# Query products in three fp32r passes and feed-forward entries on the un-normed input, in a three-block kernel on one Trainium2 core

## The chip, the core and the metric

One NeuronCore of a Trainium2 chip runs the whole program. The time is the device time of one execution in microseconds (us). The profiled execution has a time of its own, and its span (first to last instruction) is a little shorter than that.

## What is computed

The reference runs three transformer-like blocks on 256 tokens of width 1024, with 256 context tokens beside them in the first block, all in fp32. Cut to the parts that matter here:

```
mod = silu(c) @ ada_w[i] + ada_b[i]            # six vectors per block
h   = rmsnorm(x, norm1_g) * (1 + sc1) + sh1    # hc: the same of ctx
# block 0: differential attention on h and hc; block 1: short convolution
x   = x + g1 * mixer(h, hc)
x   = x + g2 * swiglu(rmsnorm(x, norm2_g) * (1 + sc2) + sh2, w_in, w_out)
# block 2: state space branch + pooling branch, then a mixture of 64 experts
```

The hidden width of both feed-forward networks (FFN) is 2816, so `w_in` is 1024 x 5632. Everything the change touches lies in the first 560 us: the query projection of block 0, and the entries to the FFN of blocks 0 and 1.

## The kernel before, in words

**Products.** Activations are held transposed, as eight tiles of 128 features by 256 tokens. An fp32 product is made as three fp32r matmuls on TensorE (`mm3`, L280 to L282): weight high part by activation high part, weight high by activation low, weight low by activation high. A weight unit (128 x 1024, eight stationary tiles) is loaded by SP into `st`, its high part `wh` is written by ScalarE (ACT, L146) and its low part `wl` by VectorE (DVE, L134). The object `st` streams the units: `take(n)` gives the next n tiles and splits some units ahead, `split_to` and `more` split further ahead, and the split instructions stand in ACT's and DVE's queue where they are issued. Ring buffers hold five split units.

**The Q stage (L591 to L660).** A loop over the eight feature tiles n adds tile n's share to the queries. It uses no split: `st.raw()` hands out the raw weights and `full`, an fp32 copy of the modulated x, and TensorE runs 8 plain fp32 matmuls for each n (L625; each leaves two records in the trace). Between them stand the products and column sums (`products`, `columns`, L504 to L524) that make the modulation vectors of a tile two ahead: 16 records into `pa`, a copy of `pa` by ACT (`pa_s`, L515), and two small matmuls into `raw` (named `ms` in the trace). `modulate_x(n + 1)` makes tile n + 1 on DVE and ACT during step n: two small sums into `ab` (L492, L493), `na` (L529), `full` (L532), `hH` (L533) and `hL` (L534). The context tile is modulated the same way by `modulate_c`, one or two tiles a step from n = 3. GpSimd (POOL) is idle there. The K stage follows, with split weights and a moving tile of 512 columns (x and context).

**The entries to the FFNs.** `residual` (L880 ff.) makes the eight output tiles of a projection and adds them to x. `done` are tiles made before it, `sums` adds up squares for the norm. For the second FFN it also feeds a `Raw` object: `Raw.split(n)` writes x times the norm's gain, un-normed, as high and low part `u`, so that products can start before the norm is known. `Raw.run` (L934 ff.) makes the first four output tiles on `u`, all four at each feature tile k, and corrects them with the row factors afterwards. The first FFN has no `Raw` before the change: it sums the squares (L351), makes 1/sqrt on DVE (L289 to L321), spreads it over rows (L363), modulates (`na` L379, `hh` L380, `hl` L383), and only then starts the products. In the background DVE works off matrix-vector units `ada` (L395), at a rate `bg_pace` for each unit of weights taken; `b.hold` keeps them back.

Of the kernel before, what the change touches and what calls it, by code (L numbers as in the profile page):

```python
# [107 lines left out]
class Stream:  # L108
# [129 lines left out]
class Builder:  # L238
# [186 lines left out]
def build(ctx, tc, ap):  # L425
# [100 lines left out]
    def modulate(src, rows, n, i, full=None):  # L526

        t = b.wk.tile([P, T], F32, tag="na", name="na", bufs=3)
        nc.vector.scalar_tensor_tensor(t, src[n], AB[n][:, 1, i:i + 1], rows, op0=ALU.mult, op1=ALU.mult)  # L529
        yield  # L530
        if full is not None:
            nc.scalar.activation(full, t, AF.Identity, bias=AB[n][:, 0, i:i + 1])  # L532
        nc.scalar.activation(hH[:, n, 1 - i], t, AF.Identity, bias=AB[n][:, 0, i:i + 1])  # L533
        nc.vector.scalar_tensor_tensor(hL[:, n, 1 - i], t, AB[n][:, 0, i:i + 1], hH[:, n, 1 - i], op0=ALU.add, op1=ALU.subtract)  # L534
        yield

    for n in ks:
        AB[n] = cp.tile([P, 2, 2], F32, name=f"ab{n}")
# [56 lines left out]
    ready, fulls = [], {}  # L595

    def modulate_x(n):
        finish_x(n)
        fulls[n] = b.wk.tile([P, T], F32, tag="rp_b", name="full", bufs=2)
        for _ in modulate(xs, rows_x, n, 0, fulls[n]):  # L600
            pass

    def modulate_c():
        todo = []
        for i in ready[:2]:
            finish_c(i)
            todo.append(modulate(cx, rows_c, i, 1))
            next(todo[-1])
        del ready[:2]
        for o in todo:  # L610
            next(o)

    modulate_x(0)
    for n in ks:
        w = st.raw()
        for i in range(KD):
            if i == 2 and n + 1 < KD:
                modulate_x(n + 1)
# [13 lines left out]
        ready.append(n)  # L632
        if n >= 3:
            modulate_c()
# [9 lines left out]
        if n >= KD - 2:  # L644
            st.nu = max(st.nu, KD)
            st.split_to(n + 3)
    while ready:
        modulate_c()
# [238 lines left out]
    def residual(ktiles, xh, xl, gate, sums, done=(), raw=None):  # L887
# [10 lines left out]
        for n in range(KD):  # L898
            if n < len(done):
                ps = done[n]  # L900
            else:
                b.hold = raw is not None and n == KD - 1
# [6 lines left out]
                if raw and n == KD - 1:  # L909
# [7 lines left out]
    class Raw:  # L917
# [3 lines left out]
        def __init__(self, A, B, pool, tag):  # L921
            self.A, self.B = A, B
# [1391 lines left out]
```

## Time and profile before

| | |
|---|---|
| time, median of 3 runs | 1554.79 us (1552.02 to 1555.33) |
| the profiled execution: time, span | 1555.31 us, 1553.5 us |
| mean granted TensorE clock | 0.989 of full speed |
| busy: TensorE, VectorE, ScalarE, GpSimd | 95%, 63%, 43%, 18% |
| Q stage, first product to first product of K | 20.9 to 62.1 us |
| first FFN, end of the residual to its 144th matmul | 232.3 to 258.0 us |
| second FFN, the same | 520.2 to 550.65 us |

A row of the timeline is: start, duration, engine, line, operation, output and inputs, shape, count, and in brackets the engine's idle time before it and what ended that. A row of a group ends with busy time, mean duration, and idle time before it. A row of windows has, after the stretch and its length, the busy time (and instructions) of PE, PEld, DVE, ACT and POOL, then the granted clock, the DMA share and GB/s; filtered by a tile it has only the engines that touch that tile.

### The profile page before, as it was taken

To read this page: it belongs to the slowest core of one execution; us is meant where nothing else is said; L and a number is where in the kernel's file an instruction comes from. 1 tells how busy PE (TensorE), PEld (TensorE's weight loads), DVE (VectorE), ACT (ScalarE), POOL (GpSimd) and SP (SyncE) were. 2 spreads that over 40 slices of the span, in tenths; PEclk is the share of its full clock that TensorE was granted. 3 is DMA by queue.
4 is the path that set the end of the run, shared out by engine and by line. 5 is a ranking of instruction groups with operands and counts; after the bars stand their busy time and mean duration, and the time that the engine had idled before them with its cause. 6 is when DMAs were issued, how large, how long until landed. Compare 5 with 4: busy or idle time off the path is not lost. (4 is left out here: it accounts for less than half of the span.)

```text
span 1553.5 us, 28280 instructions
## 1 busy us (share of the span) xinstructions
PE 1483.4 (95%) x11184; PEld 1189.5 (77%) x11184; DVE 986.0 (63%) x1850; ACT 669.0 (43%) x1175; POOL 274.2 (18%) x439
## 2 busy tenths in 40 slices
PE   6999898999999899999899999999999999999996
PEld 4789588999999899999899998999634444444332
DVE  3698858887888788796988867565423333323332
ACT  3523645444454454453677765343322222222222
POOL 0070560000100100021067668001100000000000
PEclk9999999999999899998999999999999999999999
DMA  9678215987956479786354554677489999999995
GB/s 375 232 244 273 94 69 210 340 333 283 355 201 235 172 263 350 290 325 241 126 176 162 178 176 145 218 277 301 188 303 412 420 420 420 421 420 420 421 420 215
DMA packets 71429, 431.93 MB, mean 278 GB/s; under 512 B 8176, under 2 KB 8688, under 8 KB 28416
## 3 DMA queue, kind: packets, MB, share of 16 engines
q1 hardware_dynamic: 68656, 422.77, 70.9%
q0 software_dynamic: 1344, 4.80, 0.9%
q10 hardware_dynamic: 1296, 2.55, 0.5%
q8 instruction: 88, 1.44, 0.4%
q14 instruction: 45, 0.37, 0.1%
HBM read 429.01 MB, written 1.08 MB: 277 GB/s over the span
## 5 line engine op out<-in xcount | busy, mean ns | idle before, releaser
L134 DVE TENSOR_TENSOR wl<-st,wh 128x1024 fp32r<-128x1024 f32 x294 | 365.0, 1250 | 70.4 <-ACT wh L146 70.1
L146 ACT ACTIVATE wh<-st 128x1024 fp32r<-128x1024 f32 x294 | 306.2, 1055 | 109.7 <-PE ps_r L281 41.9
L280 PE MATMUL ps_f<-hh,wh 128*128 128x256 f32 x672 | 189.2, 282 | 1.7 <-ACT hh L380 1.3
L282 PE MATMUL ps_f<-hh,wl 128*128 128x256 f32 x672 | 189.1, 281 | 0.7 <-DVE wl L134 0.7
L281 PE MATMUL ps_f<-hl,wh 128*128 128x256 f32 x672 | 189.0, 281 | 0.1
L395 DVE SCALAR_TENSOR_TENSOR ada<-ada,crow 128x1024 f32<-128x1024 f32 x128 | 164.5, 1293 | 20.4 <-DMA ada<-in_ada 20.4
L340 POOL TENSOR_TENSOR sq<-sq 128x256 f32<-128x256 f32 x30 | 38.9, 1303 | 577.8 <-ACT sq L338 577.4
L280 PEld LDWEIGHTS ps_f<-hh,wh 128*128 128x128 f32 x672 | 127.2, 189 | 2.2 <-ACT hh L380 1.5
L282 PEld LDWEIGHTS ps_f<-hh,wl 128*128 128x128 f32 x672 | 127.1, 189 | 1.0 <-DVE wl L134 1.0
L281 PEld LDWEIGHTS ps_f<-hl,wh 128*128 128x128 f32 x672 | 127.1, 189 | 0.4 <-DVE hl L383 0.4
L280 PE MATMUL ps_ssd<-hh,wh 128*128 128x256 f32 x352 | 101.4, 288 | 0.0
L281 PE MATMUL ps_r<-gL,wh 128*128 128x256 f32 x352 | 98.7, 280 | 0.0
L280 PE MATMUL ps_r<-gH,wh 128*128 128x256 f32 x352 | 98.7, 280 | 0.0
L282 PE MATMUL ps_r<-gH,wl 128*128 128x256 f32 x352 | 98.7, 280 | 0.0
L282 PE MATMUL ps_ssd<-hh,wl 128*128 128x256 f32 x352 | 98.6, 280 | 0.0
L281 PE MATMUL ps_ssd<-hl,wh 128*128 128x256 f32 x352 | 98.6, 280 | 0.0
L1818 DVE TENSOR_SCALAR xb<-gtp,A,mod 128x256 f32<-128x256 f32 (+2 forms) x52 | 27.3, 526 | 111.3 <-ACT xb L1816 111.2
L1816 ACT ACTIVATE xb<-gtp,mod,A 128x256 f32<-128x256 f32 (+2 forms) x52 | 28.5, 549 | 118.5 <-PE gtp L1836 118.4
L1806 POOL TENSOR_TENSOR WG<-G,pwq 128x256 f32<-128x256 f32 (+2 forms) x24 | 14.1, 607 | 363.5 <-DVE G L1802 363.5
L1836 PEld LDWEIGHTS gtp<-G,utH 128*128 128x128 f32 x208 | 39.2, 188 | 45.9 <-DVE xb L1818 19.7
L274 ACT ACTIVATE oH<-wr 128x512 fp32r<-128x512 f32 (+2 forms) x53 | 33.4, 630 | 92.9 <-DVE wr L2094 80.3
L280 PEld LDWEIGHTS ps_ssd<-hh,wh 128*128 128x128 f32 x352 | 66.3, 188 | 1.0 <-issue 1.0
(616 smaller groups left out, 4167.7 us busy)
## 6 DMA issues: line engine op xcount, KB each, us to landing
st<-in_ws SPq DMA_DIRECT2D x151, 1024.0 KB, 6.5
ada<-in_ada SPq DMA_DIRECT2D x128, 512.0 KB, 5.0
w<-in_we SPq DMA_DIRECT2D x40, 1024.0 KB, 19.8
w_st<-in_we SPq DMA_DIRECT2D x40, 1024.0 KB, 19.8
w_y<-in_we SPq DMA_DIRECT2D x32, 1024.0 KB, 19.8
w_ut<-in_we SPq DMA_DIRECT2D x30, 1024.0 KB, 19.8
w_h<-in_we SPq DMA_DIRECT2D x21, 1024.0 KB, 19.8
x<-in_we SPq DMA_DIRECT2D x10, 1024.0 KB, 19.8
```

The lines of the kernel that those rows point to most:

```text
L134: self.b.nc.vector.tensor_tensor(lo.rearrange("p a c -> p (a c)"), w, h.rearrange("p a c -> p (a c)"), op=ALU.subtract)
L146: nc.scalar.activation(h.rearrange("p a c -> p (a c)"), w, AF.Copy)
L274: self.nc.scalar.activation(h, src, AF.Copy)
L280: nc.tensor.matmul(out, lhsT=h[:, k], rhs=xh, start=start, stop=False, skip_group_check=True)
L281: nc.tensor.matmul(out, lhsT=h[:, k], rhs=xl, start=False, stop=False, skip_group_check=True)
L282: nc.tensor.matmul(out, lhsT=lo[:, k], rhs=xh, start=False, stop=stop, skip_group_check=True)
L340: nc.gpsimd.tensor_tensor(self.acc[tag], self.acc[tag], sq, op=ALU.add)
L395: self.nc.vector.scalar_tensor_tensor(junk, w, 1.0, crow, op0=ALU.mult, op1=ALU.mult, accum_out=dst[:, j:j + 1])
L1806: nc.gpsimd.tensor_tensor(cut(WG, tt), cut(G, tt), ws_[:, tt][:, :, None].to_broadcast([P, n, c]), op=ALU.mult)
L1816: nc.scalar.activation(out[:, k, :n], tp[:, i, :n], AF.Identity, scale=A, bias=B)
L1818: nc.vector.tensor_scalar(out[:, k, :n], tp[:, i, :n], A, B, op0=ALU.mult, op1=ALU.add)
L1836: nc.tensor.matmul(tp[:, i, :n], lhsT=hl_[:, tt, k * P:(k + 1) * P], rhs=G[:, tt, :n], start=(i == 0 and tt == 0 and hl_ is utH), stop=(tt ...
```

## The change

It has three parts. In the Q stage the weights are split and the queries are made with `mm3`; x is modulated two tiles ahead (`modulate_x(0)` and `(1)` before the loop, `modulate_x(n + 2)` after `columns(n + 2)`); the context is multiplied by its row factors by POOL after step 2, and by its gain by POOL in pairs of tiles in steps 3 to 6. The first FFN gets a `Raw` like the second. And both run by pairs: two outputs over all k, then the third, then the fourth, with the norm's sum after k = 2 of the pair. `so_out` makes two tiles ahead instead of four. `bg_pace` in the first FFN goes from 0.7 to 0.8, the slot of `ssd_norm` in the third block goes from (3, 2) to (3, 3), and the sum of squares of tile 6 takes a buffer of its own. The diff, cut:

```diff
@@ sumsq_step
-        sq = self.wk.tile([P, T], F32, tag=tag if k == 0 else "sq", name="sq", bufs=2)
+        kept = k == KD - 2
+        sq = self.wk.tile([P, T], F32, tag="na" if kept else "sq" if k else tag, name="sq", bufs=3 if kept else 2)
@@ finish_c
-        nc.scalar.activation(AB[n][:, 0, 1:2], raw[:, n, 1:2], AF.Identity, bias=b.vecs[:, ab + n:ab + n + 1])
-        nc.scalar.activation(AB[n][:, 1, 1:2], raw[:, n, 3:4], AF.Identity, bias=bsc[:, n:n + 1],
-                             scale=b.vecs[:, n1 + n:n1 + n + 1])
+        s_ = slice(n, n + 2)
+        nc.vector.tensor_tensor(ABc[:, 0, s_], raw[:, s_, 1], b.vecs[:, ab + n:ab + n + 2], op=ALU.add)
+        nc.vector.tensor_tensor(ABc[:, 1, s_], raw[:, s_, 3], b.vecs[:, n1 + n:n1 + n + 2], op=ALU.mult)
+        nc.vector.tensor_tensor(ABc[:, 1, s_], ABc[:, 1, s_], bsc[:, s_], op=ALU.add)
@@ the Q stage
     def modulate_x(n):
+        if n >= KD:
+            return
         finish_x(n)
-        fulls[n] = b.wk.tile([P, T], F32, tag="rp_b", name="full", bufs=2)
...
+        t = b.wk.tile([P, T], F32, tag="na", name="na", bufs=3)
+        nc.vector.scalar_tensor_tensor(t, x[:, n], AB[n][:, 1, 0:1], rows_x, op0=ALU.mult, op1=ALU.mult)
+        out_h(t, n, 0, AB[n][:, 0, 0:1])
+
+    def modulate_c(n):
+        finish_c(n)
+        for i in (n, n + 1):
+            nc.gpsimd.tensor_scalar(cx[i], cx[i], ABc[:, 1, i:i + 1], None, op0=ALU.mult)
+        for i in (n, n + 1):
+            out_h(cx[i], i, 1, ABc[:, 0, i:i + 1])
+    st.split_to(1)
     modulate_x(0)
+    modulate_x(1)
     for n in ks:
-        w = st.raw()
+        w = st.take(KD, 0)
         for i in range(KD):
             if i == 2 and n + 1 < KD:
-                modulate_x(n + 1)
+                st.split_to(n + 2)
...
-            nc.tensor.matmul(psq[i // 2][:, i % 2], lhsT=w[:, i], rhs=fulls[n], start=(n == 0 and i % 2 == 0), stop=(n == KD - 1),
-                             skip_group_check=True)
+            b.mm3(psq[i // 2][:, i % 2], w[i], hH[:, n, 1], hL[:, n, 1], n == 0 and i % 2 == 0, n == KD - 1)
         columns(n + 2)
+        modulate_x(n + 2)
...
         if n == 2:
             row_rstd(1, r4)
-        ready.append(n)
-        if n >= 3:
-            modulate_c()
+            rows_cs = b.wk.tile([P, T], F32, tag="rp_b", name="rows_cs", bufs=2)
+            nc.scalar.activation(rows_cs, rows_c, AF.Copy)
+            for k in ks:
+                nc.gpsimd.tensor_tensor(cx[k], cx[k], rows_cs, op=ALU.mult)
+        if 3 <= n < 7:
+            modulate_c(2 * n - 6)
@@ residual
-                b.hold = raw is not None and n == KD - 1
+                b.hold = raw is not None and n >= (KD - 1 if ktiles > KD else len(done) + 1)
...
-                if raw and n == KD - 1:
+                if raw and n == KD - 1 and not raw.pairs:
                     st.more(4)
@@ Raw
         def steps(self, outs, more):
-            w = st.take(KD * len(outs), 0)
-            for k in range(KD):
...
+            for g in ((outs[:2], *[[o] for o in outs[2:]]) if self.pairs else (outs,)):
+                w = st.take(KD * len(g), 4 - len(g) if self.pairs else 0)
+                for k in range(KD):
...
         def run(self, rstd, outs, more=None):
             go = self.steps(outs, more)
-            next(go)
+            for _ in range(3 if self.pairs else 1):
+                next(go)
             b.total()
             r = self.r = rstd()
-            st.more(5 - len(outs))
-            next(go)
-            next(go)
+            if not self.pairs:
+                st.more(5 - len(outs))
+            for _ in range(KD - 3 if self.pairs else 2):
+                next(go)
@@ the main program
-    residual(KD, oH, oL, mod(0, 2), lambda n: b.sumsq_step(ms, x[:, n], n), wo_out)
+    u0 = ExitStack()
+    raw0 = Raw(*ffn_in(0), u0.enter_context(tc.tile_pool(name="u0", bufs=1, side="right")), "u0", True)
+    residual(KD, oH, oL, mod(0, 2), lambda n: b.sumsq_step(ms, x[:, n], n), wo_out, raw0)
...
-    b.bg_pace = 0.7
+    b.bg_pace = 0.8
...
-    so_out = together([pss[i // 2][:, i % 2] for i in range(4)], rH, rL)
+    so_out = together([pss[0][:, i] for i in range(2)], rH, rL)
...
-    raw3 = Raw(*ffn_in(1), yp, "yL")
+    raw3 = Raw(*ffn_in(1), yp, "yL", True)
```

**ACT's queue in the Q loop.** Before, around steps 3 and 4 (line numbers of the kernel before; `pa_s` is the copy that the next column sums need):

```order
L515 ACTIVATE pa_s<-pa 128x256
L498 ACTIVATE ab_114<-ms,vecs 128x1
L499 ACTIVATE ab_114<-ms,bsc,vecs 128x1
L498 ACTIVATE ab_115<-ms,vecs 128x1
L499 ACTIVATE ab_115<-ms,bsc,vecs 128x1
L533 ACTIVATE hH<-na,ab_114 128x256
L533 ACTIVATE hH<-na,ab_115 128x256
```

And now, the same place (L146 is the high part of the next step's weights, L507 the copy of `pa`, L519 the high part of the activations, from `na` for x and from `cx` for the context):

```order
L146 ACTIVATE wh<-st 128x1024
L507 ACTIVATE pa_s<-pa 128x256
L519 ACTIVATE hH<-na,ab_119 128x256
L519 ACTIVATE hH<-cx,abc 128x256 x2
L626 DMA crow<-in_c 128x1024
L627 DMA crow<-in_c 128x1024
L146 ACTIVATE wh<-st 128x1024
L507 ACTIVATE pa_s<-pa 128x256
L519 ACTIVATE hH<-na,ab_120 128x256
L519 ACTIVATE hH<-cx,abc 128x256 x2
```

The context's two `hH` now stand ahead of the next step's `wh` and `pa_s`.

**POOL's queue in the Q stage.** After the change it holds, ahead of the first rotary work on `rp_b` (which stood first before):

```order
L620 TENSOR_TENSOR cx<-cx,rows_cs 128x256 x8
L592 TENSOR_SCALAR cx<-cx,abc 128x256 x8
L665 TENSOR_TENSOR rp_b<-rp_b,csts 128x256
L666 TENSOR_TENSOR qT<-qT,csts 128x256
L667 TENSOR_TENSOR qT<-qT,rp_b 128x256
```

All sixteen context operations are new on this engine; the two `hH<-cx` of a step wait for two of the eight L592.

**DVE's queue at the entry of the first FFN.** Before, from the last residual tile to the 1/sqrt:

```order
L911 SCALAR_TENSOR_TENSOR x<-ps_r,mod_92,x 128x256
L395 SCALAR_TENSOR_TENSOR ada_553,mod_92<-ada_553,crow 128x1024
L395 SCALAR_TENSOR_TENSOR ada_554,mod_92<-ada_554,crow 128x1024
L289 TENSOR_SCALAR rs_v<-ms 128x4
L307 TENSOR_SCALAR rs_r<-rs_v 128x4
```

And now (L896 is the residual, L917 the low part of `u`, L386 `ada`, L279 the start of the 1/sqrt, L370 and L374 `na` and `hl`):

```order
L917 SCALAR_TENSOR_TENSOR u<-x,A_0_95,u 128x256
L896 SCALAR_TENSOR_TENSOR x<-ps_r,mod_92,x 128x256
L917 SCALAR_TENSOR_TENSOR u<-x,A_0_95,u 128x256
L386 SCALAR_TENSOR_TENSOR ada_696,mod_92<-ada_696,crow 128x1024
L386 SCALAR_TENSOR_TENSOR ada_697,mod_92<-ada_697,crow 128x1024
L134 TENSOR_TENSOR wl<-st,wh 128x1024
L279 TENSOR_SCALAR rs_v<-ms 128x4
```

Behind the 1/sqrt now stand three `wl` before the first `na`; the `u` and one `wl` stand ahead of it.

## Rows read from the trace of the kernel before

**Rows 1.** page of before, part 1, busy us (share of the span) xinstructions, TensorE

```profile
PE 1483.4 (95%) x11184; PEld 1189.5 (77%) x11184; DVE 986.0 (63%) x1850; ACT 669.0 (43%) x1175; POOL 274.2 (18%) x439
```

**Rows 2.** timeline of PE, Q stage: start us, us, engine, line, operation, count

```profile
20.92 3.57 PE L625 MATMUL ps_q<-full,st 128*128 128x256 f32 x8 [1.55 <-ACT full L532]
...
49.47 1.97 PE L625 MATMUL ps_q<-full,st 128*128 128x256 f32 x8
...
54.69 3.70 PE L625 MATMUL ps_q<-full,st 128*128 128x256 f32 x16
...
62.14 0.58 PE L280 MATMUL ps_k<-hH,wh 128*128 128x512 f32 x1
```

**Rows 3.** windows in the first FFN: us, busy (x instructions) by engine, PEclk, DMA

```profile
260.00:300.00 40.00, 40.00 (x343) 40.00 (x342) 36.76 (x56) 21.14 (x32) 0.00 (x0) 1.00 0.95 352
```

**Rows 4.** groups by line, DVE, 10 to 75 us: xcount | busy us, mean ns

```profile
L534 DVE SCALAR_TENSOR_TENSOR hL<-na,ab,hH 128x256 fp32r<-128x256 f32 x16 | 7.5, 484 | 9.7 <-ACT hH L533 9.7
L134 DVE TENSOR_TENSOR wl<-st,wh 128x1024 fp32r<-128x1024 f32 x5 | 6.1, 1221 | 3.3 <-ACT wh L146 3.3
```

**Rows 5.** groups by line, ACT, 10 to 75 us

```profile
L533 ACT ACTIVATE hH<-na,ab 128x256 fp32r<-128x256 f32 x16 | 7.7, 497 | 2.3 <-DVE na L529 2.3
L146 ACT ACTIVATE wh<-st 128x1024 fp32r<-128x1024 f32 x6 | 6.4, 1064 | 0.0
...
L515 ACT ACTIVATE pa_s<-pa 128x256 f32<-128x256 f32 x8 | 3.0, 372 | 9.7 <-PE pa L512 9.7
```

**Rows 6.** one POOL line each: xcount: duration ns min/median/max

```profile
L831 POOL TENSOR_SCALAR od<-csts,orr x16: 609/616/665, 171.1 to 217.1; 128x128 f32<-128x128 f32 x16
...
L1364 POOL TENSOR_TENSOR xd<-sb,dtcol x16: 606/614/684, 777.3 to 927.8; 128x256 f32<-128x256 f32 x16
...
L682 POOL TENSOR_TENSOR qT<-qT,rp_b x8: 742/1602/1612, 78.2 to 121.7; 128x256 f32<-128x256 f32 x8
```

**Rows 7.** windows in the Q stage

```profile
48.00:54.00 6.00, 6.00 (x42) 4.41 (x40) 3.10 (x9) 3.76 (x12) 0.00 (x0) 1.00 0.90 280
```

**Rows 8.** waits of PE around the entry of the first FFN: us, times, longest

```profile
PE rows L363 <- DVE rs_r L321: 2.6, 1, 2.6
PE ps_f L280 <- ACT hh L380: 1.3, 1, 1.3
```

**Rows 9.** windows, products into ps_f alone, entry of the first FFN

```profile
232.30:249.10 16.80, 9.75 (x69) 9.46 (x69) 0.00 (x0) 0.00 (x0) 0.80 0.36 124
249.10:258.00 8.90, 8.90 (x77) 8.86 (x76) 0.42 (x1) 0.75 (x2) 1.00 0.45 184
```

**Rows 10.** timeline of PE, end of the first residual

```profile
232.34 0.95 PE L351 MATMUL ms<-ones,sq 128*128 128x2 f32 x8
```

**Rows 11.** timeline of DVE, entry of the first FFN

```profile
232.94 1.22 DVE L395 SCALAR_TENSOR_TENSOR ada<-ada,crow 128x1024 f32<-128x1024 f32 x1
...
239.40 0.48 DVE L383 SCALAR_TENSOR_TENSOR hl<-na,mod,hh 128x256 fp32r<-128x256 f32 x1
...
243.96 1.27 DVE L383 SCALAR_TENSOR_TENSOR hl<-na,mod,hh 128x256 fp32r<-128x256 f32 x3
```

**Rows 12.** waits of PE around the entry of the second FFN

```profile
PE ps_f L282 <- DVE wl L134: 3.9, 4, 1.8
PE ps_f L280 <- ACT wh L146: 1.4, 3, 0.6
```

**Rows 13.** windows, products into ps_f alone, entry of the second FFN

```profile
520.20:537.00 16.80, 9.95 (x44) 8.41 (x45) 0.00 (x0) 0.00 (x0) 0.70 0.64 240
537.00:550.65 13.65, 12.47 (x103) 12.06 (x102) 0.88 (x4) 0.00 (x0) 1.00 0.00 1
```

**Rows 14.** windows, clock: second FFN's entry, then the third block's entry

```profile
526.00:536.00 10.00, 9.54 (x44) 9.24 (x44) 4.71 (x17) 1.76 (x3) 0.00 (x0) 0.50 0.56 204
725.00:726.00 1.00, 0.47 (x5) 0.47 (x5) 0.00 (x0) 0.42 (x1) 0.00 (x0) 1.00 0.92 381
728.00:737.00 9.00, 9.00 (x41) 8.66 (x41) 3.10 (x16) 0.57 (x2) 0.00 (x0) 0.50 0.02 7
```

More of the change, by code (lines that the diff above doesn't have):

```diff
@@ L524, in columns, with out_h @@
                              skip_group_check=True)
[L526 to L535, printed above, removed]
+    def out_h(t, n, i, o):
+        nc.scalar.activation(hH[:, n, 1 - i], t, AF.Identity, bias=o)
+        nc.vector.scalar_tensor_tensor(hL[:, n, 1 - i], t, o, hH[:, n, 1 - i], op0=ALU.add, op1=ALU.subtract)
     for n in ks:
-        AB[n] = cp.tile([P, 2, 2], F32, name=f"ab{n}")
+        AB[n] = cp.tile([P, 2, 1], F32, name=f"ab{n}")
+    ABc = cp.tile([P, 2, KD], F32, name="abc")
     nc.scalar.activation(bsc[:, :2], b.ones2, AF.Silu)
@@ L917, in build, with __init__ @@
     class Raw:
-        def __init__(self, A, B, pool, tag):
-            self.A, self.B = A, B
+        def __init__(self, A, B, pool, tag, pairs=False):
+            self.A, self.B, self.pairs = A, B, pairs
             u = pool.tile([P, 2, KD, T + 2], F32R, tag=tag, name="u", bufs=1)
@@ L981, in mod, with ffn_in @@
         return mods[i][:, 8 * p:8 * p + 8]
+    def ffn_in(i):
+        b.need((f"L{i}", 4))
+        b.make_A("norm2_g", 8 * i, mods[i], 4, A2[i])
+        return A2[i], mod(i, 3)
     ms = b.new_ms()
-    residual(KD, oH, oL, mod(0, 2), lambda n: b.sumsq_step(ms, x[:, n], n), wo_out)
+    u0 = ExitStack()
+    raw0 = Raw(*ffn_in(0), u0.enter_context(tc.tile_pool(name="u0", bufs=1, side="right")), "u0", True)
+    residual(KD, oH, oL, mod(0, 2), lambda n: b.sumsq_step(ms, x[:, n], n), wo_out, raw0)
     b.ada_last = ada2
@@ L998, in project, with ffn @@
             b.mm3(out, w[k], hh[:, k], hl[:, k], first and k == 0, k == KD - 1)
-    def ffn_in(i):
-        b.need((f"L{i}", 4))
-        b.make_A("norm2_g", 8 * i, mods[i], 4, A2[i])
-        return A2[i], mod(i, 3)
-    def ffn(i, ms, sums, after, raw=None):
-        key = f"L{i}"
-        if raw:
-            rps = [p.tile([P, 512], F32, tag=t, name="ps_f") for p, t in ((b.aux, "aux"), (b.ps, "ps")) for _ in range(2)]
-            hh, hl = raw.run(lambda: b.rstd_cols(ms[:, 0:4], 4, 1.0 / D, b.wk), rps)
-        else:
-            hh, hl = modulated(b.rstd_rows(ms), *ffn_in(i))
+    def ffn(i, ms, sums, after, raw):
+        key = f"L{i}"
+        rps = [p.tile([P, 512], F32, tag=t, name="ps_f") for p, t in ((b.aux, "aux"), (b.ps, "ps")) for _ in range(2)]
+        hh, hl = raw.run(lambda: b.rstd_cols(ms[:, 0:4], 4, 1.0 / D, b.wk), rps)
+        u0.close()
         fs = ExitStack()
@@ L1032, in glu @@
             nc.vector.tensor_tensor(gL[:, j], s, gH[:, j], op=ALU.subtract)
-        if raw:
-            for _ in glu(0, rps[0], rps[1]):
-                pass
-            steps = glu(1, rps[2], rps[3])
-        else:
-            pss = [b.ps.tile([P, 512], F32, tag="ps", name="ps_f") for _ in range(2)]
-            together([o for ps in pss for o in (ps[:, :T], ps[:, T:])], hh, hl)
-            for _ in glu(0, pss[0]):
-                pass
-            steps = glu(1, pss[1])
+        ps = b.ps.tile([P, 512], F32, tag="ps", name="ps_f")
+        together([ps[:, :T], ps[:, T:]], hh, hl)
+        for _ in glu(0, rps[0], rps[1]):
+            pass
+        for _ in glu(1, rps[2], rps[3]):
+            pass
+        steps = glu(2, ps)
         sums = sums()
-        for j in range(2, KFF):
+        for j in range(3, KFF):
             ps = b.ps.tile([P, 512], F32, tag="ps", name="ps_f")
@@ L1131, in build @@
     b.need(("L1", 2))
-    pss = [b.ps.tile([P, 2, T], F32, tag="ps", name="ps_so") for _ in range(2)]
-    so_out = together([pss[i // 2][:, i % 2] for i in range(4)], rH, rL)
+    pss = [b.ps.tile([P, 2, T], F32, tag="ps", name="ps_so")]
+    so_out = together([pss[0][:, i] for i in range(2)], rH, rL)
     ms2 = b.new_ms()
-    raw3 = Raw(*ffn_in(1), yp, "yL")
+    raw3 = Raw(*ffn_in(1), yp, "yL", True)
     residual(KD, rH, rL, mod(1, 2), lambda n: b.sumsq_step(ms2, x[:, n], n), so_out, raw3)
```

37 lines of the change are left out of this document (7 added, 30 removed).

## The prediction

> **What bounds the kernel now.** I first read the page: TensorE is busy 95% of the span [rows 1], so what counts is where it does work that could be cheaper, or waits. Then I read the three places of the change in the timeline, the waits and the windows. In full flow a three-pass product issues a matmul every 40/343 = 0.117 us, with TensorE never idle [rows 3]; that is the yardstick below.
>
> In the Q stage TensorE is the bound too: from 20.92 to 62.14 us it works nearly without a gap, a step takes 54.69 - 49.47 = 5.2 us, and the sixteen records of one step's eight fp32 matmuls take 3.7 us of it, less some 0.2 us of overlap at the end [rows 2]. VectorE is busy half of that time and POOL not at all [rows 7].
>
> At the two FFN entries TensorE waits. The first 144 matmuls of an FFN (six outputs, eight k, three passes) would take 144 x 0.117 = 16.8 us without a gap. In the first FFN they take from 232.3 to 258.0 us [rows 9], 8.9 us too long: 2.6 us of waiting for the 1/sqrt and 1.3 us for the first modulated tile [rows 8], some 1.5 us of sums and rows, and the rest at a lowered clock (mean 0.80 in the first 16.8 us [rows 9]). In the second they take 30.45 us, to 550.65 [rows 13], 13.7 us too long: 3.9 us of waits for low and 1.4 us for high parts of weights [rows 12], and ten microseconds in which the granted clock was 0.50, the lower of its two levels [rows 14].
>
> **Part 1, the Q stage: +12 us (+8 to +16).** *Removed:* eight matmuls of 3.5 us net per step, and `full`. *Added:* 24 matmuls of 0.117 = 2.8 us, so TensorE alone would need 5.2 - 0.7 = 4.5 us a step; had nothing else changed, this would save about 4 us over the first six steps. But each step now also needs a `wl` on VectorE (1.22 us [rows 4]) and a `wh` on ScalarE (1.06 us [rows 5]), and ScalarE's queue has them in a chain. In steps 3 to 6 the two `hH` of the context stand ahead of the next `wh` and `pa_s`, and they wait for POOL. So from one `columns` to the next the path is: the two small sums and `na` on VectorE (some 0.9 us), `hH` 0.50, `hL` 0.48, three small sums for the context 0.5, the way to POOL 0.2 (my estimate), two POOL operations of length T, the last `hH` 0.50, `wh` 1.06, `pa_s` 0.37, `columns` 0.6 [rows 4, 5]; with the starts of neighbours overlapping that is about 5.6 + 2T. A step that waits on it is longer than TensorE's 4.5 us for any T above zero.
>
> *The price of T.* The trace has no POOL operation of this form on 256 columns. The nearest are a tensor-scalar on 128 columns at 0.616, a two-input operation on 256 columns at 0.614, and the same at 1.602 us (0.742 at the shortest) [rows 6]. The last stands in the K stage, where VectorE is nearly always at work. The bounds are thus 0.6 and 1.6. I take 0.95 for the tensor-scalar, since 0.616 is for half its columns and some of it is a fixed start, and since VectorE waits for POOL while it runs; for the eight products with the row factors, which run beside a working VectorE, 0.85.
>
> The slow end has this sentence beside it: the Trainium skill, SBUF — State Buffer, section "Who interferes with whom", says that a VectorE operation with two inputs in SBUF contends with a POOL operation that reads SBUF and that the later one blocks entirely, and the spread 0.742 to 1.602 agrees. By that rule alone, with every POOL operation at the slow price, part 1 would be about +20 us; this is rival 2.
>
> *Running the steps through* with these durations, in queue order: step 1 begins at 28.0. Column sums 3 wait for a `pa_s` that stands behind eight squares of the context and a `wh` on ScalarE, which costs 2.1 us (step 2 at 34.8). Steps 3 and 4 begin at 41.2 and 45.9, about 1.7 us late. POOL's eight products run from 42.7 to 49.5 and hold up the first pair, so step 5 begins at 53.9 (before 49.47), step 6 at 61.4 (before 54.69), step 7 at 68.0, the K stage at 73.6 (before 62.14 [rows 2]): +11.4, and its first `wl` is 0.8 later behind its `wh` than before: +12. Each 0.1 us more or less of a POOL operation moves this by about 1.2 us (sixteen operations, not all on the path): 0.62 for all gives +8, and 0.15 more for the scalars gives +13.4. Above that +16 allows for a lowered clock after one of the new gaps of 2 to 3.5 us. A stage that is late here stays late: the K stage is TensorE-bound and nothing behind it waits for a fixed date.
>
> **Part 2, first FFN: -3.3 us (-6 to +2).** The un-normed pair can start at 232.3, at the end of the residual [rows 10]: its first 18 matmuls fill 2.1 us that were idle. The sum then waits for the last square, whose x is behind a `wl` and a `u` on VectorE; I get its end at 235.9, and the pair's other 30 matmuls end at 239.4. The 1/sqrt starts behind both `ada` (1.22 us each [rows 11]) and a `wl`, so the row factors come at about 241.2: 1.9 us of waiting stay. Outputs 3 and 4 then take 48 x 0.117 = 5.6 us, to 247.5. Three more `wl` stand ahead of `na`, so the first `hl` ends near 248.4; the eight `hl` took from 239.4 to 245.2 [rows 11], so the last is ready near 253.7 and matmul 144 ends at 254.4 instead of 258.0. That is -3.6, less 0.3 for the row product and correction on VectorE. If the clock does not fall I can gain up to 6; if it falls in the new wait, a stretch of ten microseconds at the lower level costs five, which gives +2.
>
> **Part 3, second FFN: -10.6 us (-12.5 to -7).** Two residual tiles ahead instead of four leave the queues of VectorE and ScalarE more time for each `wl` and `u`; the new order has one x, one `wl`, one `u` in turn, 2.2 us against the residual tile's 24 x 0.117 = 2.8. So the waits for weights of 3.9 and 1.4 us [rows 12] go and so does the slow clock: the pair ends near 522.3, the sum takes 1.5, the rest of the pair to 527.3, the row factors cost 0.6, outputs 3 and 4 follow, and the first `hl` comes about 0.8 late: matmul 144 ends near 540 instead of 550.65 [rows 13]. The clock is the risk: at 725 us one microsecond of half idleness was followed by nine at 0.50 [rows 14].
>
> **The rest: +0.5 us (0 to +1).** The pace 0.8 moves background work earlier in the first FFN, where VectorE is busy 36.8 of 40 us with TensorE at 40 of 40 [rows 3]; if that cover were gone, each extra operation would cost up to 1.2 us. The moving tile of 258 instead of 256 columns adds under 1% to 96 matmuls. The buffer of the sixth square takes a POOL wait away that lies beside matmuls. The slot in the third block I cost at nothing.
>
> **Sum.** +12 - 3.3 - 10.6 + 0.5 = -1.4 us. The profiled execution took 1555.3, 0.5 above the median of 1554.8; so 1553.9, which I give as 1554.0. A measurement can tell about 0.2%, 3.1 us, from no change: under 1551.7 is faster, over 1557.9 slower.
>
> **Rivals.**
> 1. *The Q loop stays with TensorE.* If POOL's operations take 0.6 us and ScalarE keeps ahead, only the early squares and a late step or two cost: +4, so 1555.3 + 4 - 13.4 = 1546. For it: VectorE and ScalarE are half idle there [rows 7]. Against: the chain of 5.6 + 2T is longer than 4.5 even then. Chance 0.2.
> 2. *POOL at its contended price, slower than before.* If the sixteen operations take 1.2 to 1.5 us, the pairs hold ScalarE's queue, and with it `pa_s` and `wh`, 5 to 9 us longer: +17 to +21, giving 1559 to 1563. For it: the 1.602 median [rows 6]. Against: it was measured beside a full VectorE. It decides from a mean of about 1.2 us. Chance 0.17.
> 3. *An entry keeps its gap.* If the clock falls at the first FFN's wait for the row factors, or the second still waits for its weights, 6 to 8 us of parts 2 and 3 do not come: 1561. For it: the clock fell after a pause as short as that at 725 us [rows 14]. Chance 0.13.
>
> **How the numbers follow.** My forecast has 0.5 and reaches from 1548 to 1560. Faster: all of rival 1 and a third of the forecast, 0.37. Slower: rivals 2 and 3, less what ends under the line, and a little of the forecast, 0.29. Same: 0.34. The range 1545 to 1562 takes in rival 1, most of rival 3 and half of rival 2; about 0.15 is left out.
>
> **What would show it.** In the changed profile the K stage should start near 73.6; TensorE's waits in the Q stage should be for `pa_s` at steps 2, 5, 6 and for `wh` at step 7; POOL's tensor-scalar should read about 0.95. In the first FFN the row product should wait about 2 us for the 1/sqrt and the clock stay at 1.00; in the second no wait for `wl` over 0.5 us and matmul 144 about 20 us after the residual. I am wrong if steps 5 and 6 take under 5.5 us, if POOL takes over 1.2, or if the windows behind either entry show a clock of 0.50.

## The result: 0.6% slower

| | before | after |
|---|---|---|
| time, median of 6 runs (range) | 1552.13 us (1548.96 to 1555.33) | 1562.2 us (1559.95 to 1565.32) |
| profiled execution: span | 1553.5 us | 1563.5 us |
| granted clock, mean | 0.989 | 0.987 |

The ratio is 1.0057 with a 95% interval of 1.0037 to 1.0077: slower by 5.7 to 12.0 us. The forecast was 1554.0 with a range of 1545 to 1562. TensorE is as busy as in [rows 1], in a span that is 10 us longer (page, part 1, of after):

```profile
PE 1487.6 (95%) x11248; PEld 1193.0 (76%) x11248; DVE 1004.5 (64%) x1880; ACT 672.6 (43%) x1171; POOL 290.3 (19%) x455
```

Where the 10 us come from shows in the start times of the same matmuls in both timelines. The table has what each stretch adds to the lateness against the kernel before, and what the sum of the prediction said:

| stretch, up to | before, us | shift in the change | this stretch adds | forecast |
|---|---|---|---|---|
| K stage, first matmul | 62.1 | +14.4 | +14.4 | +12 |
| first residual | 221.0 | +17.6 | +3.2 | 0 |
| first FFN, 144th matmul | 258.0 | +15.5 | -2.1 | -3.3 |
| convolution, 48th matmul | 437.0 | +26.8 | +11.4 | +0.5 |
| second FFN, first product | 520.2 | +26.5 | -0.4 | 0 |
| second FFN, 144th matmul | 550.6 | +16.9 | -9.5 | -10.6 |
| third block, its output projection | 1065.4 | +10.0 | -6.9 | 0 |

**The Q stage.** Timeline of PE in the changed kernel, the rows that answer to [rows 2]: the start of the stage, the waits of 2.29 us (step 2), 1.02 (before step 3), 3.11 (step 5) and 2.84 (step 7), step 6 at 64.88 us, and the K stage's first matmul.

```profile
21.97 0.58 PE L270 MATMUL ps_q<-hH,wh 128*128 128x256 f32 x1 [2.29 <-ACT hH L519]
...
35.81 0.61 PE L515 MATMUL ms<-csts,pa_s 128*128 128x2 f32 x4 [2.29 <-ACT pa_s L507]
...
44.67 0.71 PE L569 MATMUL rows<-csts,rs_r 128*128 128x128 f32 x4 [1.02 <-DVE na L586]
...
56.98 0.61 PE L515 MATMUL ms<-csts,pa_s 128*128 128x2 f32 x4 [3.11 <-ACT pa_s L507]
...
64.88 0.36 PE L270 MATMUL ps_q<-hH,wh 128*128 128x256 f32 x1
...
71.10 0.39 PE L270 MATMUL ps_q<-hH,wh 128*128 128x256 f32 x1 [2.84 <-ACT wh L146]
...
76.52 0.40 PE L270 MATMUL ps_k<-hH,wh 128*128 128x512 f32 x1
```

The wait of 3.11 us is explained by ScalarE's timeline just before it. The two `hH` of the context wait for POOL, and `wh` and `pa_s` stand behind them:

```profile
53.80 0.51 ACT L519 ACTIVATE hH<-cx,abc 128x256 fp32r<-128x256 f32 x1 [2.56 <-POOL cx L592]
54.72 0.51 ACT L519 ACTIVATE hH<-cx,abc 128x256 fp32r<-128x256 f32 x1 [0.41 <-POOL cx L592]
...
55.59 1.06 ACT L146 ACTIVATE wh<-st 128x1024 fp32r<-128x1024 f32 x1 [0.36 <-issue]
56.56 0.37 ACT L507 ACTIVATE pa_s<-pa 128x256 f32<-128x256 f32 x1
```

POOL's groups from 40 to 76 us give the price that [rows 6] had bounded: 0.92 and, in the mean, 0.88 us.

```profile
L592 POOL TENSOR_SCALAR cx<-cx,abc 128x256 f32<-128x256 f32 x8 | 7.3, 924 | 14.7 <-DVE abc L492 14.7
L620 POOL TENSOR_TENSOR cx<-cx,rows_cs 128x256 f32<-128x256 f32 x8 | 6.7, 884 | 45.4 <-ACT rows_cs L618 45.4
```

Windows show what followed. Behind each of the three long waits the granted clock (third number from the right) fell to near its lower level for some 4 us, and once more at 219 us:

```profile
38.00:42.00 4.00, 4.00 (x28) 2.57 (x29) 3.18 (x15) 1.29 (x3) 0.00 (x0) 0.57 1.01 422
...
58.00:62.00 4.00, 4.00 (x27) 2.51 (x28) 1.69 (x8) 1.01 (x2) 1.70 (x2) 0.57 0.90 345
...
72.00:76.00 4.00, 3.64 (x18) 3.64 (x19) 1.58 (x6) 1.84 (x3) 1.82 (x2) 0.57 0.68 217
...
219.00:226.00 7.00, 6.68 (x32) 6.14 (x30) 2.09 (x7) 1.46 (x3) 5.55 (x21) 0.51 0.01 2
```

Below, "lost to the clock" is the sum, over windows of 1 us up to 1100 us, of TensorE's busy time times (1 - granted clock). In the Q stage it is 5.0 us, where before had none; at 219 us 3.3. At the start of the stage the matmuls run at about half their later rate in both kernels (before, 8 records in 3.57 us and later 8 in 1.97 [rows 2]) at a granted clock that reads 1.00, so that is not in these sums.

**The two FFN entries.** Products into `ps_f` alone; against [rows 9] and [rows 13] the 144 matmuls now take 23.6 and 20.8 us (25.7 and 30.4 before), at a clock of 1.00 throughout:

```profile
249.85:266.65 16.80, 12.54 (x97) 11.77 (x97) 0.00 (x0) 0.00 (x0) 1.00 0.59 232
266.65:273.60 6.95, 6.70 (x48) 5.98 (x48) 0.00 (x0) 0.00 (x0) 1.00 0.31 124
```

```profile
546.70:563.50 16.80, 15.12 (x115) 14.04 (x115) 0.00 (x0) 0.00 (x0) 1.00 0.48 172
563.50:567.60 4.10, 4.10 (x31) 3.65 (x31) 0.00 (x0) 0.00 (x0) 1.00 0.00 0
```

The first FFN's entry has the waits that were foreseen in place of [rows 8] (waits of PE, 225 to 275 us):

```profile
PE rows L942 <- DVE rs_r L311: 1.5, 1, 1.5
PE ms L342 <- ACT sq L329: 0.9, 1, 0.9
PE ps_f L271 <- DVE hl L374: 0.3, 1, 0.3
```

**Between them** lies the surprise. From 275 to 460 us, the rest of the first FFN and the convolution's entry, the same view names no wait at all for the kernel before, and for the changed one:

```profile
PE ps_cu L272 <- DVE wl L134: 1.6, 1, 1.6
PE ms L342 <- ACT sq L329: 1.3, 1, 1.3
PE ps_f L272 <- DVE wl L134: 1.2, 3, 0.5
PE ps_r L272 <- DVE wl L134: 0.5, 1, 0.5
PE ps_b L272 <- DVE wl L134: 0.5, 1, 0.5
...
```

VectorE is late. Its last background operation before the convolution began at 416 us before, 11 us ahead of the convolution's first product (427.1); in the change at 447 us, 1 us ahead (448.3). Timeline of DVE and of PE, two rows of before, then two of the change:

```profile
415.79 1.22 DVE L395 SCALAR_TENSOR_TENSOR ada<-ada,crow 128x1024 f32<-128x1024 f32 x1
427.08 0.28 PE L280 MATMUL ps_cu<-u,wh 128*128 128x258 f32 x1
...
447.45 1.23 DVE L386 SCALAR_TENSOR_TENSOR ada<-ada,crow 128x1024 f32<-128x1024 f32 x1 [0.75 <-DMA ada<-in_ada]
448.30 0.28 PE L270 MATMUL ps_cu<-u,wh 128*128 128x258 f32 x1
```

VectorE is not simply full. In this stretch (258.0 to 437.0 us before, 273.5 to 463.8 in the change) it is busy 152 and 161 us, and its waits with a background operation at the head of its queue, for that operation's own load, grow from 9.4 to 23.0 us (waits of DVE, before and after):

```profile
DVE ada L395 <- DMA ada<-in_ada: 9.4, 9, 2.3
...
DVE ada L386 <- DMA ada<-in_ada: 23.0, 22, 2.7
```

### The profile page after: what moved, and what is told of

Same layout as the page of the kernel before. It is cut to its first block, busy times and chain, and to the rows that moved or that the text cites. A ratio compares the mean times of both kernels' runs of the same rounds, so it can differ in the third digit from the quotient of the medians.

```text
span 1563.5 us, 28452 instructions
## 1 busy us (share of the span) xinstructions
PE 1487.6 (95%) x11248; PEld 1193.0 (76%) x11248; DVE 1004.5 (64%) x1880; ACT 672.6 (43%) x1171; POOL 290.3 (19%) x455
## 5 line engine op out<-in xcount | busy, mean ns | idle before, releaser
L134 DVE TENSOR_TENSOR wl<-st,wh 128x1024 fp32r<-128x1024 f32 x302 | 377.1, 1257 | 72.2 <-ACT wh L146 71.8
L146 ACT ACTIVATE wh<-st 128x1024 fp32r<-128x1024 f32 x302 | 313.6, 1054 | 94.5 <-DMA st<-in_ws 30.0
L386 DVE SCALAR_TENSOR_TENSOR ada<-ada,crow 128x1024 f32<-128x1024 f32 x128 | 164.9, 1295 | 31.2 <-DMA ada<-in_ada 30.9
L272 PE MATMUL ps_f<-hh,wl 128*128 128x256 f32 x640 | 180.4, 282 | 1.3 <-DVE wl L134 1.2
L271 PE MATMUL ps_f<-hl,wh 128*128 128x256 f32 x640 | 181.0, 283 | 0.5 <-DVE hl L374 0.5
L270 PE MATMUL ps_f<-hh,wh 128*128 128x256 f32 x640 | 180.0, 281 | 0.3
L271 PEld LDWEIGHTS ps_f<-hl,wh 128*128 128x128 f32 x640 | 120.6, 188 | 2.4 <-DVE hl L374 1.4
L272 PEld LDWEIGHTS ps_f<-hh,wl 128*128 128x128 f32 x640 | 120.6, 188 | 2.3 <-DVE wl L134 2.3
L270 PEld LDWEIGHTS ps_f<-hh,wh 128*128 128x128 f32 x640 | 120.6, 188 | 0.7 <-ACT hh L371 0.7
```

The costliest lines, as they stand in the source:

```text
L134: self.b.nc.vector.tensor_tensor(lo.rearrange("p a c -> p (a c)"), w, h.rearrange("p a c -> p (a c)"), op=ALU.subtract)
L146: nc.scalar.activation(h.rearrange("p a c -> p (a c)"), w, AF.Copy)
L270: nc.tensor.matmul(out, lhsT=h[:, k], rhs=xh, start=start, stop=False, skip_group_check=True)
L271: nc.tensor.matmul(out, lhsT=h[:, k], rhs=xl, start=False, stop=False, skip_group_check=True)
L272: nc.tensor.matmul(out, lhsT=lo[:, k], rhs=xh, start=False, stop=stop, skip_group_check=True)
L386: self.nc.vector.scalar_tensor_tensor(junk, w, 1.0, crow, op0=ALU.mult, op1=ALU.mult, accum_out=dst[:, j:j + 1])
```

## The experiments

Each was timed beside the kernel before on the same chip; ratios are to it.

### The Q stage alone, and all but the Q stage

The edits are the hunks of the diff: for `q_only` those of `finish_c` and the Q stage on the kernel before, for `no_q` all the others.

> The kernel before with the Q stage of the change alone (split weights, three fp32r passes, context on POOL). Theory: the Q stage costs 14 us by itself, so the time is 13 to 16 us above the kernel before, the K stage starts near 76.5 us, and everything from 260 us on runs as in the kernel before, shifted. Rival: part of the loss that the changed kernel shows at the attention's end and in the first FFN follows from the Q stage (other background work, another phase of the clock); then the time is 18 us or more above before.

> The changed kernel with the Q stage of the kernel before. Theory: without the 14 us of the Q stage it is 14 to 16 us faster than the changed kernel, 4 to 6 us faster than the kernel before; the entry of the second FFN still gains 9.5 us, that of the first 2, and the stretch from the first FFN to the convolution's entry still loses about 11. Rival: the 11 us there come from the late Q stage and go with it; then it is 15 us or more faster than before.

`q_only`: 1.0086 (1.006 to 1.0111), 13 us slower on the medians. The K stage starts 14.6 us late, and behind it the shift stays between 17.8 and 21.0 until the third block: the theory holds, with 3.2 us lost in the falling clock at 219 us on top. `no_q`: 0.9945 (0.9925 to 0.9964), 8.5 us faster on the ratio, more than the 4 to 6 expected. The stretch to the convolution still loses 10.4 us, and the second FFN's entry gains 9.5, so the rival falls: that loss does not come from the Q stage.

### The background pace

```diff
-    b.bg_pace = 0.8
+    b.bg_pace = 0.7
```

> The changed kernel with the background pace of the first FFN at 0.7 as before. Theory: the pace of 0.8 fills VectorE and makes the low parts of weights late from 280 us to the convolution's entry at 456 us; with 0.7 those waits go and the time falls by 8 to 11 us against the changed kernel, to about the time before. Rival: the waits come from the moved holds and the un-normed entry, not from the pace; then less than 3 us change. Where background work is left over, up to 3 us of it may come back later.

And the other way, on the kernel before, `b.bg_pace` from 0.7 to 0.8 and nothing else:

> The kernel before with the pace of 0.8 in the first FFN and nothing else. Theory: the pace alone fills VectorE before the convolution's entry, so from the first FFN's 144th matmul to the 48th matmul of the convolution it loses 4 to 9 us against before; some of it may come back at the third block's entry, where no background work is left. Rival: VectorE has room for the pace as long as the first FFN's un-normed parts and the holds are not there; then under 2 us are lost there.

`pace07`: 1.0094 (1.0067 to 1.012), not the gain that was expected. In its place the theory was right: from the first FFN's 144th matmul to the convolution's 48th it adds 2.0 us instead of 11.4, with one wait of 0.2 us in that stretch. But the work is not gone. Seven background operations were left at the third block's entry (one in the change, two before). There TensorE waits 13.8 us, and that entry adds 12.5 us where the change gains 2.3. Waits of PE, 700 to 780 us, and the piece of VectorE's timeline behind it, where each `ada` waits for its own load:

```profile
PE ps_ssd L272 <- DVE wl L134: 13.8, 1, 13.8
```

```profile
752.08 1.23 DVE L386 SCALAR_TENSOR_TENSOR ada<-ada,crow 128x1024 f32<-128x1024 f32 x1 [2.54 <-DMA ada<-in_ada]
...
756.95 1.22 DVE L386 SCALAR_TENSOR_TENSOR ada<-ada,crow 128x1024 f32<-128x1024 f32 x1 [2.04 <-DMA ada<-in_ada]
```

`pace08`: 1.0024 (1.0003 to 1.0045); the stretch adds 5.6 us, and from the residual to its end VectorE begins 53 background operations instead of 46. Of the 5.6, 3.7 come between the convolution's first and 48th product, from waits and the clock. The other 1.9 are no waits: in the first FFN TensorE's matmuls follow one another every 118.7 ns in this execution and every 117.3 in that of before. So the pace alone does somewhat over a third of the damage. In the change, where the un-normed tiles of the first FFN come on top, it is 9.4 (11.4 less 2.0).

### The slot in the third block

One number in the change, and the reverse in the kernel before:

```diff
-    SLOTS = [(ssd_norm, 3, 3), (ssd_exp, 1, 5),
+    SLOTS = [(ssd_norm, 3, 2), (ssd_exp, 1, 5),
...
```

> The changed kernel with the slot of the state space norm at (3, 2) as before. Theory: the slot (3, 3) is what takes 5 gaps of some 1.5 us out of the third block between 810 and 910 us; with (3, 2) they return and the time rises by 3.5 to 6 us. Rival: those gaps went because less background work or another phase was left there; then no change.

> The kernel before with the slot of the state space norm at (3, 3) and nothing else. Theory: the five waits of TensorE for POOL's 1/sqrt between 810 and 910 us, 4.0 us in all before and 0.4 in the change, go with the slot, and 3 to 4 us of time with them. Rival: with (3, 3) the norm is ready in time but what it delays costs as much; then no change in the time.

`slot32`: 1.0055 (1.0033 to 1.0076), beside 1.0057 of the change: no difference in the time. `slot33`: 0.9986 (0.9969 to 1.0002), 2 us that are within the uncertainty. Neither time can tell 3 us from nothing, so the rise expected of `slot32` and the gain expected of `slot33` are not shown by them. The traces are plain, though. Waits of PE from 800 to 930 us, before and with the slot alone:

```profile
PE rows_s L1405 <- POOL rs_r L305: 4.0, 5, 1.2
```

```profile
PE rows_s L1405 <- POOL rs_r L305: 0.5, 1, 0.5
```

The change has 0.4 us there, `slot32` 3.4. And the work itself comes sooner. From the first to the fifth group of `xt` matmuls in the third block it is 87.1 us before and 83.7 with the slot alone (timeline of PE, two rows of before, then two of `slot33`):

```profile
775.62 0.60 PE L1359 MATMUL xt<-csts,sb 128*128 128x128 f32 x4
862.71 0.60 PE L1359 MATMUL xt<-csts,sb 128*128 128x128 f32 x4
...
773.82 0.60 PE L1359 MATMUL xt<-csts,sb 128*128 128x128 f32 x4
857.51 0.60 PE L1359 MATMUL xt<-csts,sb 128*128 128x128 f32 x4
```

All nine kernels with the slot at (3, 3) take 82.9 to 83.7 us there, all five with (3, 2) 86.7 to 87.1. So the slot gives some 3.4 us of the third block's gain.

### The chain in the Q stage

`q_order` issues the context pairs a step later, behind `wh` and `pa_s`; `q_dve` gives the sixteen operations to VectorE at their old places.

```diff
+            if i == 6 and n >= 4:
+                modulate_c(2 * n - 8)
...
-        if 3 <= n < 7:
-            modulate_c(2 * n - 6)
```

> The changed kernel with the context pairs issued one step later, after the products of the next step, so that ScalarE's queue has wh and pa_s ahead of the context's two hH. Theory: the Q stage is long because wh and pa_s stand behind operations that wait for POOL; with the order turned the steps from the fifth on take 4.7 to 5.2 instead of 7.4 us, the K stage starts 6 to 9 us earlier than 76.5, and the time falls by as much. Rival: POOL's own duration sets the pace, in whatever order; then the K stage moves by less than 2 us.

```diff
-            nc.gpsimd.tensor_scalar(cx[i], cx[i], ABc[:, 1, i:i + 1], None, op0=ALU.mult)
+            nc.vector.tensor_scalar(cx[i], cx[i], ABc[:, 1, i:i + 1], None, op0=ALU.mult)
...
-                nc.gpsimd.tensor_tensor(cx[k], cx[k], rows_cs, op=ALU.mult)
+                nc.vector.tensor_tensor(cx[k], cx[k], rows_cs, op=ALU.mult)
```

> The changed kernel with the context's sixteen POOL operations given to VectorE, at the same places in the program. Theory: a step of the chain is 5.6 + 2T us with T the duration of a context operation; on VectorE T is about 0.3 instead of 0.92 and the way to another engine falls away, so steps 4 to 7 shorten by about 1.4 us each and the K stage starts 4 to 7 us earlier than 76.5. Rival: POOL is not in the chain, and the eight products and eight scalings on VectorE only delay wl there; then the K stage moves by less than 1 us or comes later.

`q_order`: 1.0043 (1.0021 to 1.0066), K stage at 71.96 us, 4.6 earlier; `q_dve`: 1.0019 (0.9995 to 1.0043), K stage at 71.98, 4.5 earlier. Both the place in ScalarE's queue and the engine of the context's work matter; T fell from 0.92 to 0.35 us, and the way to a third engine went with it (groups of VectorE in `q_dve`):

```profile
L620 DVE TENSOR_TENSOR cx<-cx,rows_cs 128x256 f32<-128x256 f32 x8 | 2.8, 421 | 0.2 <-ACT rows_cs L618 0.2
L592 DVE TENSOR_SCALAR cx<-cx,abc 128x256 f32<-128x256 f32 x8 | 2.5, 351 | 0.1
```

`q_order` stayed short of its 6 to 9 us, and a new wait stands in its place (waits of PE, 18 to 85 us): the column sums write to a tile of which VectorE's `abc` still reads another part, and `abc` stands behind the context's `hL`.

```profile
PE ms L515 <- DVE abc L491: 3.2, 2, 2.8
```

### Versions without the Q stage, and a better one

`f1_only` is the kernel before with the second FFN's part alone. `f_pace` is `no_q` with other paces; `ffn_best` changes them again and holds the background work one tile earlier; `all_best` is `ffn_best` with a rearranged three-pass Q stage.

The edit of `f1_only`, beside the change's own hunks of `Raw.steps` and `Raw.run`:

```diff
-    b.bg_pace = 0.7
+    b.bg_pace = 0.75
...
-    so_out = together([pss[i // 2][:, i % 2] for i in range(4)], rH, rL)
+    so_out = together([pss[0][:, i] for i in range(2)], rH, rL)
...
-    raw3 = Raw(*ffn_in(1), yp, "yL")
+    raw3 = Raw(*ffn_in(1), yp, "yL", True)
```

> The kernel before with the third part alone: the second FFN by pairs, two residual tiles ahead, and the pace after the convolution at 0.75 so that no background work piles up at the third block. Theory: the entry of the second FFN gains 9.5 us as in the changed kernel and nothing else moves, so 8 to 10 us faster than before. Rival: the gain there needs the other parts (the clock falls at that entry without them); then less than 5 us.

`f_pace`, from `no_q`:

```diff
-    b.bg_pace = 0.8
+    b.bg_pace = 0.7
...
-    b.bg_pace = 0.25
+    b.bg_pace = 0.4
...
-    b.bg_pace = 0.7
+    b.bg_pace = 0.75
```

> The changed kernel with the Q stage of before, and the background work spread otherwise: pace 0.7 in the first FFN, 0.4 instead of 0.25 in the convolution, 0.75 instead of 0.7 after it, so that one background operation is left at the third block's entry as in the change. Theory: the convolution's entry waits for low parts of weights because the pace of 0.8 fills VectorE before it; here its 6.8 us and some 2 of the 2.8 us inside the first FFN come back, so it is 7 to 9 us faster than the change without its Q stage, 14 to 17 us faster than before. Rival: the waits are those of the un-normed entry with its holds, and the work moved into the convolution costs there what it saves; then within 3 us of the change without its Q stage.

`ffn_best`, also from `no_q`:

```diff
-    b.bg_pace = 0.8
+    b.bg_pace = 0.75
...
-                b.hold = raw is not None and n >= (KD - 1 if ktiles > KD else len(done) + 1)
+                b.hold = raw is not None and n >= (KD - 2 if ktiles > KD else len(done) + 1)
...
-    b.bg_pace = 0.25
+    b.bg_pace = 0.4
...
-    b.bg_pace = 0.7
+    b.bg_pace = 0.75
```

> The changed kernel with the Q stage of before, pace 0.75 in the first FFN, 0.4 in the convolution, 0.75 after it, and the background work held back from the last two instead of the last one output tile of either FFN. Theory: VectorE then has caught up when the convolution and the third block begin, so neither entry waits for low parts of weights; 4 to 6 us faster than with the first spreading of the background work, 14 to 17 us faster than before. Rival: the work held back is lacking later and two operations at the third block's entry cost what is saved; then within 2 us of the first spreading.

And `all_best`, with these paces and this hold, from the change (its Q stage, with the context on VectorE as in `q_dve`):

```diff
+    pairs_at = {(5, 6): 0, (6, 6): 2, (7, 2): 4, (7, 6): 6}
...
-            if i == 2 and n == 2:
+            if i == 6 and n == 2:
                 total(1, accs_c)
-            if i == 5 and n == 2:
                 r4 = rstd_of(1)
...
+            if i == 5 and n == 1:
+                accs_c = sums(cx)
+            if (n, i) in pairs_at:
+                modulate_c(pairs_at[n, i])
...
         columns(n + 2)
+        if n == 3:
+            row_rstd(1, r4)
         modulate_x(n + 2)
+        if n >= 3 and n < 7:
+            finish_c(2 * n - 6)
```

> The last kernel, but with a three-pass Q stage rearranged: context work on VectorE and behind wh and pa_s, the context's squares a step later, the context's row factors ahead of na. Theory: without the chain a step takes 4.5 to 4.9 us, the K stage starts between 60 and 66 us, near the 62 of before: three passes then cost nothing, but the gain is at most 2 us. Rival: the start of TensorE after short waits lowers the clock also here, and VectorE and ScalarE stay late; then the K stage starts after 68 us.

`f1_only`: 0.9977 (0.996 to 0.9993), 3.6 us instead of 8 to 10. Its entry gains 5.6 us, not 9.5: four waits of 0.3 us for `hl` stand there, and the clock fell with the last of them.

```profile
537.00:545.00 8.00, 7.70 (x37) 7.09 (x37) 6.75 (x16) 3.40 (x6) 0.00 (x0) 0.57 0.01 2
```

So the rival has half the truth: in its profiled execution the part alone did not keep the clock. All nine kernels with both FFN parts kept it there, in one profiled execution each.

`f_pace`: 0.9922 (0.9892 to 0.9952), 12 us faster than before and 3.6 us faster than `no_q` on the ratios, where 14 to 17 and 7 to 9 were expected. The stretch to the convolution adds 0.6 instead of the 10.4 us of `no_q`, as the theory said. But the third block's entry, where `no_q` gains 2.3, loses 4.2: VectorE is late again, now there, and after a wait of 2.2 us for x the clock was low for 15 us.

```profile
718.00:733.00 15.00, 15.00 (x76) 14.66 (x75) 5.07 (x22) 2.79 (x7) 0.00 (x0) 0.54 0.25 86
```

`ffn_best`: 0.9911 (0.9889 to 0.9934), 13.8 us faster than before on the ratio. This is the lowest ratio of all. The entries of the convolution and of the third block run without a wait for `wl`, only 3.4 us are lost to the clock up to 1100 us (12.2 before), and of the waits for `wl` between 225 and 760 us this is left:

```profile
PE ps_f L282 <- DVE wl L134: 0.5, 2, 0.3
```

The 4 to 6 us expected against `f_pace` are not shown: the ratios differ by 1.7 us and the intervals overlap. In the traces it is ahead by 4.2 us at the third block's output projection (-15.0 and -10.8).

`all_best`: 0.9928 (0.9907 to 0.9948). Its Q stage has the context on VectorE, behind `wh` and `pa_s`, the squares of the context a step later and the row factors ahead of `na`. The K stage starts at 63.54 us (62.14 before), and no clock fall is left in the Q stage. Three passes cost 1.4 us there, then, and not 14.4, but they gain nothing: the waits that remain are those for the halves of the weights, for the start, and one of the column sums (waits of PE, 18 to 85 us).

```profile
PE ps_q L270 <- ACT hH L519: 2.3, 1, 2.3
PE ps_q L272 <- DVE wl L134: 1.9, 2, 1.1
PE ms L515 <- DVE rs_v L279: 1.1, 1, 1.1
PE ps_q L270 <- ACT wh L146: 0.9, 1, 0.9
```

## Why the prediction was wrong

**The step that failed is "The rest: +0.5 us".** It took the pace of 0.8 for work moved to where VectorE is 36.8 of 40 us busy [rows 3], and priced an extra operation at up to 1.2 us, its own duration, and that only if the cover were gone. The stretch to the convolution lost 11.4 us. The row itself said that the cover was thin: 3.2 us free in 40. What the step left out is that background work stands in VectorE's queue ahead of `wl`, and waits there for its own load. Those waits are 21.6 to 25.4 us in that stretch in all six kernels with the pace of 0.8, and 3.4 to 19.2 in the other eight. So an extra operation does not cost its duration here and there: a backlog is carried on to the next entry, where every `wl`, x and square is on the path, and TensorE's pauses cost clock besides (1.6 us at 454 us). The fourteen traces agree on it. In eight of them the last background operation begins 10.8 us or more ahead of the convolution's first product, and the first 48 products there lose nothing; in the six with 0.8 it begins 2.8 us ahead at most, and 3.7 to 9.3 us are lost. With 0.7 in the change 9.4 of the 11.4 us go; with 0.8 alone in the kernel before 3.7 come. How much of the backlog is the loads and how much the number of operations was not separated: no run changed the loads alone.

That the change needs the higher pace was missed too: its longer holds take slots from the background work, and what is not done in time stops the third block for 13.8 us.

Of the 11.4 us, 5.6 are TensorE's waits and 1.6 the clock. Another 1.4 are the interval between matmuls that wait for nothing: 118.3 ns in the change's execution and 117.3 in that of before, so 340 instead of 344 of them stand in 40 us at a clock of 1.00. The rest are the matmuls right behind the waits, which come further apart. Windows without a wait, before and after:

```profile
385.00:425.00 40.00, 40.00 (x344) 40.00 (x343) 35.09 (x47) 19.79 (x27) 6.12 (x5) 1.00 0.91 347
...
400.00:440.00 40.00, 40.00 (x340) 40.00 (x339) 33.77 (x48) 16.64 (x23) 4.96 (x4) 1.00 0.90 328
```

The interval is 118.3 ns in `pace07` as well and makes most of its 2.0 us. What sets it stays open.

**Part 1, +12 us, measured +14.4.** The mechanism was right, and so were the places: waits for `pa_s` at steps 2, 5 and 6 and for `wh` at step 7, and POOL's tensor-scalar at 0.92 for an estimate of 0.95. Step by step, the stage is late at its start and in step 2, and not in the chain. Step 1 began at 29.3 instead of 28.0, 1.1 of it because the first product came later (21.97, before 20.92). Step 2 took 8.9 us instead of 6.4: the row products waited 1.0 us for `na`, which reads another part of the same tile, and the clock fell (1.7 us lost at 38 us). Steps 3 to 7 took 31.4 us for a forecast of 32.4, though the two other falls lie in them. And of the +12, 0.8 was for a wait behind the K stage's first matmul that is not in the 14.4 and measured 0.3. The clock fell three times in every profiled execution with this Q stage as written, for 5.0 to 9.4 us in all. The prediction had it only in the range ("up to +16"), although [rows 14] showed a fall after half a microsecond of idleness.

Two of its numbers came out right for other reasons than those given. The terms listed for the chain add up to 5.1 + 2T, not 5.6 + 2T, and overlap could only shorten that; step 5 took 7.44 us, which is 5.6 + 2 x 0.92, because the list leaves out 0.24 us between the column sums and VectorE and 0.36 us of ScalarE ahead of `wh`. And the 0.85 for the eight products is a mean that none of them had: six took 0.73 to 0.74 us, one 0.91 and one 1.73. Rival 2, POOL at its contended price, did not come, though the time lies where it put it. Rival 1 is refuted: POOL and ScalarE's queue are in the chain.

The rule of the Trainium skill that was weighed (SBUF — State Buffer, "Who interferes with whom") is borne out where the two engines met: the product of 1.73 us is the one that ran beside a `wl` on VectorE, and that `wl` took 1.61 us instead of 1.23. The last product, of 0.91 us, began beside an `hL` that took 0.76 us instead of 0.48. Those are two of POOL's sixteen operations. Rows of POOL and of VectorE in the change:

```profile
47.26 1.73 POOL L620 TENSOR_TENSOR cx<-cx,rows_cs 128x256 f32<-128x256 f32 x1
...
46.78 1.61 DVE L134 TENSOR_TENSOR wl<-st,wh 128x1024 fp32r<-128x1024 f32 x1 [1.11 <-ACT wh L146]
```

**Part 2, -3.3 us, measured -2.1, and part 3, -10.6 us, measured -9.5.** Both terms hold in mechanism and nearly in size: the wait for the row factors is 1.5 us for 1.9, and both clocks stayed at 1.00. In part 2 the norm's sum ended 1.0 us later against the residual than forecast, since it waited 0.9 us for the last square, and what follows is later by about as much. Rival 3 did not come in the change.

**What the sum did not have.** The third block gains 6.9 us. The slot that was costed at nothing, which lies there and not in the first 560 us, gives 3.4 of them; the block's entry gives 2.3, since it lost 3.4 instead of 5.1 us to the clock, though 1.7 went a little later; the cause of the remaining 1.2 stays open. And the 3.2 us between the K stage and the residual are mostly the fall of the clock at 219 us (3.3 us). It follows a wait of 1.85 us that the kernel before has as well, without a fall. `q_only` has the fall too, `pace07` and `slot32` with the same Q stage do not: it comes and goes between executions.

## What to carry to other kernels

An engine that is 90% busy beside a saturated TensorE had no room for background work near a serial entry, and less where that work waited for its own loads at the head of the queue: look at when the last such operation begins against the entry, and at what it waits for, not at the engine's mean share. Work that is held back somewhere has to be found a place elsewhere, so count what is left over at the point that needs it all. And on an in-order queue, issue what the bottleneck waits for ahead of what itself waits for a third engine.

## What was not expected of the hardware

- A wait of TensorE of 2 to 3 us in the Q stage was followed within some 3 us by about 4 us at a granted clock of 0.57, three times in the change. In `f1_only` a fall came with the last of four waits of 0.3 us. A wait of 1.85 us ahead of the first residual was followed by one in the change and not before.
- The clock loses 3.4 to 21.0 us of an execution over the fourteen traces, and 15.0 and 21.0 in the change and `slot32`, which differ in one number. A difference of 3 us in a stretch of a single trace is weak evidence here; one that separates all fourteen traces, as at the convolution's entry, is not.
- Matmuls that wait for nothing follow one another every 117.3 ns in some stretches and executions and every 118.3 or 118.7 in others, at a granted clock of 1.00. Over the 1526 matmuls from the first FFN to the convolution that is 1.5 to 2 us.
- TensorE waits for reads by other engines of other parts of the tile that it writes (1.0 us for `na`, up to 2.8 us for `abc`).
